# Hybrid mLSTM and gated DeltaNet layer: 512-wide token-major projections, weight units begun from ScalarE's queue, and new places of the chain in TensorE's order

## The chip, the cores and the metric

One core of a Trainium2 chip runs the whole layer as one program. The metric is the device time in microseconds, the median of the runs; less is better.

## The reference, cut to what matters

One decoder layer over 2048 tokens with 1024 features, all in float32. The normalised input is multiplied with one wide input projection. Its columns feed four mLSTM heads (q, k of 128, v, o, z of 256 columns a head) and eight gated DeltaNet heads (q, k, v with a short causal convolution, and a gate z). Both recurrences run chunk by chunk; the outputs are normalised and gated and go through one output projection.

```
h = rms_norm(x, attn_norm); proj = h @ w_in
mq, mk, mv, mo, mz, mi, mf, gqkv, gz, gb, ga = split(proj)
h_m = mlstm_chunkwise(mq, mk, mv, mi, mf)
y_m = rms(h_m) * m_out_norm * sigmoid(mo) * silu(mz)
gq, gk, gv = split(silu(causal_conv(gqkv)))
o_g = gated_delta_chunkwise(l2(gq), l2(gk), gv, log_alpha(ga), sigmoid(gb))
y_g = rms(o_g) * g_out_norm * silu(gz)
out = rms_norm(x + concat(y_m, y_g) @ w_out, final_norm)
```

## The kernel before

The tokens are taken in four segments of 512 (four tiles of 128). Each segment runs eight windows in turn: a P window for each pair of DeltaNet heads (projections gk, gq, gv with the convolution, and gz) and an M window for each mLSTM head (mq and mk, then mv, mo, mz). A projection in float32 is made of three products of rounded parts: weights high and low, input high and low (`hh`, `hl`).

There are two kinds of projection. Feature-major ones (`proj_fm`, names pf_) hold the weights as the stationary operand and stream 512 tokens. Token-major ones (`proj_tm`, names pt_: gz, mv, mo, mz) hold 128 tokens and stream 256 weight columns, one token tile after the other; each tile takes 24 matmuls (8 k by 3 products) into one of three projection banks (`psj`, bufs=3). When a tile is done, ScalarE and VectorE evict it: `gate` in `m_proj` (lines 545 to 547) for mz, line 539 for mo, `keep_v` (lines 528, 536) for mv, `gate` in `g_proj_z` (lines 723, 724) for gz.

TensorE's order is written out by hand. `window` runs through the steps of a window's projections and sums their planned costs; at given shares of the planned total `WIN` it puts in a step of another stream: the DeltaNet preparation (`prep`), the inversion levels (`lvl`, places from `LV0` to `LV1`), the DeltaNet chain (`chain`) and the mLSTM chunks (`mch`). A chunk of the chain has three steps: `sp` (state times key) from which VectorE makes the residual R out of `vr` (line 974); `vq` (line 980), which ScalarE copies to V; and `su` and `op` (lines 991 to 998), from which the state and the output follow. The places of the chain are evenly spaced, six in the P window from `CH0` and the others in the M window from 0.02 to `CH1`. A level's matmuls zp, fp, zq, fq (lines 906 to 932) alternate with copies and transposes (dmz) on the other engines. The other engines' order comes from the framework's list scheduler, in which streams with `PRI` go ahead of the window's own evictions.

The weights are split into high and low parts once, in segment 0, and stored to DRAM. From segment 1 on, `load_w` (line 157) reads them back through SP's queue, four units of 512 KB for a group of 256 columns, into a ring of ten units, one group ahead of use. SP's queue also carries all other loads and the stores of y.

Of the kernel before, what the change touches and what calls it, by code (L numbers as in the profile page):

```python
# [17 lines left out]
P = 128  # L18
# [47 lines left out]
def hybrid_layer(  # L66
# [79 lines left out]
    parts_d = {}  # L146

    def unit(ncol, dt, nm):
        return wp.tile([P, HK, ncol], dt, tag="wu", name=nm, bufs=10)

    def load_w(key, src, ncol, nm, between=None):

        if key in parts_d:
            his, los = ([unit(ncol, F32R, f"{p_}_{nm}_{i}") for i in range(2)] for p_ in ("whi", "wlo"))
            for i in range(2):
                for part, t_ in enumerate((his[i], los[i])):
                    nc.sync.dma_start(t_.bitcast(F32), parts_d[key][part, i])
            return his, los
        return split_w(key, src, ncol, nm, between)

    def split_w(key, src, ncol, nm, between):

        raws = [unit(ncol, F32, f"wraw_{nm}_{i}") for i in range(2)]
        step = 2 if between else HK
        for k in range(0, KT, step):
            nc.sync.dma_start(raws[k // HK][:, k % HK:k % HK + step, :], src[:, k:k + step, :])
# [13 lines left out]
        kept = parts_d[key] = ypool.tile([2, 2, P, HK, ncol], F32, tag=f"wd{nm}", name=f"wd{nm}")  # L180
        for i in range(2):
            for part, t_ in enumerate((his[i], los[i])):
                nc.sync.dma_start(kept[part, i], t_.bitcast(F32))
        return his, los

    wloads = []
    for seg in range(NSEG):
        for kind, n in ORDER_LAST if seg == NSEG - 1 else ORDER:
            for i in range(4) if kind == "M" else (3, 1, 0, 2) if n == 0 else (1, 0, 2, 3):
                nm, key = f"{kind}{seg}_{n}_{i}", (kind, n, i)  # L190
                if kind == "M":
                    wloads.append((key, wg[n * 4 + i], 256, nm))
                elif (n, i) == (0, 3):
                    wloads.append((key, wgz, 256 + NG, nm))
                else:
                    wloads.append((key, wg[16 + n * 4 + i - (n > 0)], 256, nm))
    wready, nloads = [], len(wloads)

    def prefetch_w(between=None):
        if wloads:  # L200
            wready.append(load_w(*wloads.pop(0), between))

# [141 lines left out]
    def proj_fm(w, c0, nm, done):  # L344

        hi, lo = w
        ps = psj.tile([P, T], F32, tag="pj", name=f"pf_{nm}")
        for k in range(KT):
            nc.tensor.matmul(ps, lhsT=hi[k // HK][:, k % HK, c0:c0 + P], rhs=hh[k], start=(k == 0), stop=False)  # L349
            nc.tensor.matmul(ps, lhsT=hi[k // HK][:, k % HK, c0:c0 + P], rhs=hl[k], start=False, stop=False)  # L350
            nc.tensor.matmul(ps, lhsT=lo[k // HK][:, k % HK, c0:c0 + P], rhs=hh[k], start=False, stop=(k == KT - 1))
            if k == KT - 1:
# [3 lines left out]
    def tm_step(ps, w, t, k):  # L356
        hi, lo = (p_[k // HK][:, k % HK, :] for p_ in w)
        ts = slice(t * P, (t + 1) * P)
# [21 lines left out]
    def proj_tm(w, nm, done, scaled=True):  # L380

        n = w[0][0].shape[-1]
        for t in range(NCH):
            ps = psj.tile([P, T], F32, tag="pj", name=f"pt_{nm}_{t}")[:, 0:n]
            for k in range(KT):
                tm_step(ps, w, t, k)
                if k == KT - 1:
                    tm_done(ps, t, done, scaled)
                yield 0.33

    def proj_tm_first(w, nm, done):

        n = w[0][0].shape[-1]
        pss = [psc.tile([P, T], F32, tag="cp", name=f"pt_{nm}_{t}")[:, 0:n] for t in range(NCH)]
        for k in range(KT):
            for t in range(NCH):
                tm_step(pss[t], w, t, k)
            if k == KT - 1:
                rms_first()
# [103 lines left out]

    def m_proj(seg, n, r):
        s_ = f"{seg}_{n}"
        w = next_w()
        qT = wk.tile([P, T], F32, tag="mq", name=f"mq{s_}")
# [4 lines left out]
        r.update(q=qT, k=kT, v=vt, g=G)  # L512
        yield from proj_fm(w, 0, f"mq{s_}",
                           lambda ps: fm_out(qT, ps, DK ** -0.5))
        yield from proj_fm(w, P, f"mk{s_}", lambda ps: fm_out(kT, ps))
        w = next_w()
        if fast:
# [6 lines left out]
        def keep_v(ps, t):  # L524
# [4 lines left out]
            if fast:  # L529
                v_ = vt[:, t, 0:256].bitcast(F32)  # L530
                with tc.high_priority(VPR):
# [3 lines left out]
                    else:  # L535
                        nc.vector.tensor_tensor(vlo[:, t, :], ps, v_, op=ALU.subtract)  # L536
        yield from proj_tm(w, f"mv{s_}", keep_v, False)
        w = next_w()
        yield from proj_tm(w, f"mo{s_}", lambda ps, t: nc.scalar.activation(
            G[:, t, :], ps, AF.Tanh, scale=rs0h[:, t:t + 1] if raw[0] else 0.5), False)  # L540
        w = next_w()

        def gate(ps, t):
# [127 lines left out]
    def g_proj(seg, pr, r, st):  # L671
# [3 lines left out]
        yield from g_proj_qkv(seg, pr, r)  # L675
        if pr:
            yield from g_proj_z(seg, pr, r, st)
# [33 lines left out]

    def g_proj_z(seg, pr, r, st):
        s_ = f"{seg}_{pr}"
        w = next_w()
        G = wkp.tile([P, NCH, 256], F32, tag="gg", name=f"gg{s_}", bufs=2)
# [5 lines left out]
        def gate(ps, t):  # L721
# [4 lines left out]
            if pr == 0:  # L726
# [209 lines left out]
    def g_chain(seg, pr, r, st):  # L936
# [158 lines left out]
    for _ in range(NWARM):  # L1095
        nc.tensor.matmul(warm_ps[:, 0:P], lhsT=ones, rhs=ones, start=True, stop=True)
    lvl, chain, mch = {}, {}, {}
    st = None
    for seg in range(NSEG):
# [17 lines left out]
        for kind, n in ORDER_LAST if last else ORDER:  # L1117
            r = {}
            streams, keep = [], ()
            if kind == "P":  # L1120
# [19 lines left out]
                window(g_proj(seg, n, r, st), WIN, streams, keep)  # L1140
                lvl[n], chain[n] = g_level(seg, n, r), g_chain(seg, n, r, st)
# [3 lines left out]
            else:  # L1145
# [256 lines left out]
```

## Time and profile before

| | |
|---|---|
| median of 3 runs (lowest, highest) | 2298.92 us (2297.42, 2300.68) |
| profiled execution, its time | 2303.72 us |
| its span | 2301.9 us |
| TensorE busy | 2213.8 us, 14798 matmuls |
| VectorE / ScalarE / GpSimd busy | 1837.0 / 854.7 / 796.9 us |
| mean granted TensorE clock | 0.984 |

Busy time is the union of an engine's instructions; matmuls overlap each other, and their ends are modelled. A row of waits gives how long an engine stood idle ahead of an instruction, and whose result ended the wait.

### The profile page before, as it was taken

The numbers are of one execution on the slowest core, as the hardware profiler recorded it, in microseconds if no ns is written. First come the engines' busy times: TensorE is split into PE (matmuls) and PEld (weight loads), VectorE is DVE, ScalarE is ACT, GpSimd is POOL, SyncE is SP. The second block draws the span as 40 slices with busy tenths as digits, with TensorE's granted clock in tenths as the row PEclk, the third lists the DMA queues.
The fourth block names the chain that finished last, engine by engine and source line by source line (L and its number), as shares of the span: only waits on it lengthen the run. The fifth ranks groups of instructions, "written<-read, shape, count | busy, mean of one in ns | idle before, by whom it ended". The sixth has DMA issues, their size and how long they took to land.

```text
span 2301.9 us, 41838 instructions
## 1 busy us (share of the span) xinstructions
PE 2213.8 (96%) x14798; PEld 1965.1 (85%) x14798; DVE 1837.0 (80%) x5168; ACT 854.7 (37%) x2293; POOL 796.9 (35%) x1220
## 2 busy tenths in 40 slices
PE   8899999989999999989999999999999999999998
PEld 7779888887889898979898989888988997788787
DVE  7887878788897979789888898698767737877784
ACT  5445545525242434352424243434244234111111
POOL 4656555652121212421111114221111114555543
PEclk9999999999999999999999999999999999999999
DMA  7766766754546464644454546554546555232321
GB/s 274 257 232 224 248 225 245 256 201 163 191 154 202 144 210 158 229 162 165 145 197 157 199 156 232 167 179 163 181 167 204 174 171 163 73 101 92 101 83 64
DMA packets 183322, 409.19 MB, mean 178 GB/s; under 512 B 51736, under 2 KB 84632, under 8 KB 183112
## 3 DMA queue, kind: packets, MB, share of 16 engines
q1 hardware_dynamic: 182392, 405.74, 51.9%
q8 instruction: 116, 1.90, 0.3%
q14 instruction: 94, 0.77, 0.1%
q10 hardware_dynamic: 720, 0.79, 0.1%
HBM read 309.68 MB, written 96.90 MB: 177 GB/s over the span
## 4 chain that ended last, share of the span: by engine, by line
PE 60%; DVE 24%; DMA 8%; ACT 3%; issue 2%; POOL 2%; SPq 1%; ACTq 0%; POOLq 0%; DVEq 0%
PE po L1258 5%; PE po L1257 5%; PE po L1256 5%; DVE xb L850 3%; DVE tb L846 3%; DVE kw L500 2%; DVE ktok L500 2%; PE pt_gz L361 2%; PE pt_gz L359 2%; PE pt_gz L360 2%; PE pt_mz L359 2%; PE pt_mz L360 2%; PE pt_mz L361 2%; PE pf_gv L349 2%; PE pf_gv L350 2%
## 5 line engine op out<-in xcount | busy, mean ns | idle before, releaser
L1217 DVE STREAM_TRANSPOSE ytt<-yl 32x256 f32<-32x256 f32 x448 | 195.3, 436 | 45.3 <-POOL ylo L1185 39.3
L1014 POOL TENSOR_TENSOR gms<-gms,nhalf 128x2 f32<-128x2 f32 x64 | 47.4, 740 | 410.9 <-DVE gms L1012 408.6
L846 DVE TENSOR_TENSOR tb<-xb,lbt 128x248 f32<-128x248 f32 (+30 forms) x496 | 167.1, 337 | 20.7 <-DMA lbt<-l_d 7.9
L850 DVE TENSOR_TENSOR xb<-xb,tb 128x248 f32<-128x248 f32 (+30 forms) x496 | 168.4, 339 | 12.8
L359 PE MATMUL pt_mv<-whi_M,hh 128*128 128x256 f32 x512 | 150.7, 294 | 8.3 <-DVE mk L371 3.9
L359 PE MATMUL pt_gz<-whi_P,hh 128*128 128x256 f32 (+1 forms) x512 | 152.6, 298 | 4.3 <-ACT hh L337 2.5
L359 PE MATMUL pt_mz<-whi_M,hh 128*128 128x256 f32 x512 | 149.6, 292 | 3.1 <-DVE tz L546 3.1
L359 PE MATMUL pt_mo<-whi_M,hh 128*128 128x256 f32 x512 | 148.7, 290 | 3.2 <-DVE vlo L536 3.2
L361 PE MATMUL pt_gz<-whi_P,hl 128*128 128x256 f32 (+1 forms) x512 | 147.8, 289 | 1.6 <-DVE hl L338 1.6
L360 PE MATMUL pt_gz<-wlo_P,hh 128*128 128x256 f32 (+1 forms) x512 | 147.7, 288 | 1.7 <-DVE wlo_P L178 1.7
L360 PE MATMUL pt_mv<-wlo_M,hh 128*128 128x256 f32 x512 | 147.2, 287 | 0.0
L361 PE MATMUL pt_mv<-whi_M,hl 128*128 128x256 f32 x512 | 146.9, 287 | 0.0
L360 PE MATMUL pt_mz<-wlo_M,hh 128*128 128x256 f32 x512 | 145.4, 284 | 0.0
L361 PE MATMUL pt_mz<-whi_M,hl 128*128 128x256 f32 x512 | 145.3, 284 | 0.0
L360 PE MATMUL pt_mo<-wlo_M,hh 128*128 128x256 f32 x512 | 144.2, 282 | 0.0
L361 PE MATMUL pt_mo<-whi_M,hl 128*128 128x256 f32 x512 | 144.2, 282 | 0.0
L1265 ACT ACTIVATE jkf<-xr 128x512 f32<-128x512 f32 (+1 forms) x33 | 20.4, 619 | 271.5 <-DVE xr L1263 148.1
L1256 PE MATMUL po<-woh,yh 128*128 128x512 f32 (+1 forms) x297 | 114.6, 386 | 1.6 <-ACT yh L1183 1.6
L1258 PE MATMUL po<-woh,ylo 128*128 128x512 f32 (+1 forms) x297 | 114.7, 386 | 0.1
L178 POOL TENSOR_TENSOR wlo_M<-wraw_M,whi_M 128x256 fp32r<-128x256 f32 x128 | 97.4, 793 | 49.3 <-ACT whi_M L175 48.7
L1257 PE MATMUL po<-wol,yh 128*128 128x512 f32 (+1 forms) x297 | 114.3, 385 | 0.0
L359 PEld LDWEIGHTS pt_mv<-whi_M,hh 128*128 128x128 f32 x512 | 100.0, 195 | 10.5 <-DVE mk L371 4.3
(408 smaller groups left out, 7539.4 us busy)
## 6 DMA issues: line engine op xcount, KB each, us to landing
whi_M<-wdM SPq DMA_DIRECT2D x96, 512.0 KB, 4.1
wlo_M<-wdM SPq DMA_DIRECT2D x96, 512.0 KB, 5.2
whi_P<-wdP SPq DMA_DIRECT2D x90, 512.0 KB, 3.9
wlo_P<-wdP SPq DMA_DIRECT2D x90, 512.0 KB, 4.7
wraw_M<-in_wg_dram SPq DMA_DIRECT2D x32, 512.0 KB, 5.9
wdM<-whi_M SPq DMA_DIRECT2D x32, 512.0 KB, 3.2
wdM<-wlo_M SPq DMA_DIRECT2D x32, 512.0 KB, 5.2
wraw_P<-in_wg_dram SPq DMA_DIRECT2D x30, 512.0 KB, 5.6
```

What stands on the lines that cost most here:

```text
L178: eng.tensor_tensor(lo[:, ks, :], raw_[:, ks, :], hi[:, ks, :].bitcast(F32), op=ALU.subtract)
L359: nc.tensor.matmul(ps, lhsT=hh[k][:, ts], rhs=hi, start=(k == 0), stop=False)
L360: nc.tensor.matmul(ps, lhsT=hh[k][:, ts], rhs=lo, start=False, stop=False)
L361: nc.tensor.matmul(ps, lhsT=hl[k][:, ts], rhs=hi, start=False, stop=(k == KT - 1))
L500: nc.vector.transpose(dst[32 * a:32 * a + 32, :, 32 * b:32 * b + 32], s4[32 * b:32 * b + 32, :, a, :])
L846: nc.vector.tensor_tensor(tb[:, :, 0:n], xb[:, :, i:i + 1].broadcast_to([P, 8, n]), lbt[:, i:i + 1, i + 1:32].broadcast_to([P, 8, n]), op= ...
L850: nc.vector.tensor_tensor(xs, xs, tb[:, :, 0:n], op=ALU.subtract)
L1014: nc.gpsimd.tensor_tensor(ms, ms, nhalf[:, 0:2], op=ALU.pow)
L1217: nc.vector.transpose(ytt[32 * b:32 * b + 32, :, 32 * a:32 * a + 32], y3[32 * a:32 * a + 32, :, 32 * b:32 * b + 32])
L1256: nc.tensor.matmul(ps, lhsT=yh, rhs=woh, start=(k == 0), stop=False)
L1257: nc.tensor.matmul(ps, lhsT=yh, rhs=wol, start=False, stop=False)
L1258: nc.tensor.matmul(ps, lhsT=ylo, rhs=woh, start=False, stop=(k == 15))
```

## The change

Four things are done. (1) From segment 1 on, mo and mz of a head are one projection of 512 columns, and, for the seven head pairs of `wide_z`, gz and mv too; gz then leaves the P window and stands with mv at the start of the M window, ahead of mq and mk. `proj_tm_wide` takes two token tiles at a time, k in the outer loop, into two of the three banks. The planned window lengths become 31.0 (P) and 52.0 (M) where gz moves. The paired weights are stored side by side in DRAM. (2) From segment 1 on, weight units are loaded by ScalarE's queue, each where TensorE's order has just released a unit of the ring (`pump`, `freed`). (3) The places of levels, chain, last mLSTM steps and gate steps are given one by one: longer gaps behind steps that VectorE follows, shorter behind those that ScalarE follows. (4) The chain's residual R is written in the place of `vr`, which gets two buffers.

```diff
-LV0, LV1, CH0, CH_N, CH1 = (0.26, 0.42, 0.44, 6, 1.0)
+NU = 10
+LVP, LVW = (0.26, 0.3, 0.34, 0.4, 0.45), (0.2, 0.24, 0.29, 0.34, 0.41)
+CHP = (0.42, 0.46, 0.63, 0.71, 0.88)
+CHM = (0.03, 0.11, 0.28, 0.45, 0.53, 0.7, 0.87, 0.95)
+CWP = (0.44, 0.5, 0.7, 0.82)
+CWM = (0.01, 0.15, 0.22, 0.36, 0.5, 0.57, 0.71, 0.85, 0.92)
-MC2 = (0.0, 0.1, 0.15, 0.195, 0.2)
+MC2 = (0.0, 0.1, 0.18, 0.25, 0.32)
-GP, RB = ((0.4, 0.9, 0.97), 0.31)
+GP, RB = ((0.4, 0.82, 0.97), 0.31)
-LVA = (0.26, 0.45, 0.47, 1.03)
+LVA = ((0.26, 0.3, 0.345, 0.41, 0.46), 0.47, 1.03)
...
+        if isinstance(key, list):
+            w = Weights(nm, 512, 2)
+            kept = parts_d[key[0]][0]
+            w.due = [((p_, i), kept[p_, i // 2, :, i % 2 * 2:i % 2 * 2 + 2]) for i in range(4) for p_ in range(2)]
+        else:
+            kept, c0, n = parts_d[key]
+            w = Weights(nm, n, HK)
             for i in range(2):
-                for part, t_ in enumerate((his[i], los[i])):
-                    nc.sync.dma_start(t_.bitcast(F32), parts_d[key][part, i])
-            return his, los
-        return split_w(key, src, ncol, nm, between)
+                for p_ in range(2):
+                    w.due.append(((p_, i), kept[p_, i, :, :, c0:c0 + n]))
+        return w
+
+    def pump():
+        while coming and ring["free"] > 0:
+            w = coming[0]
+            at, src = w.due.pop(0)
+            t_ = w.units[at] = unit_(w.rows, w.n, F32R, f"w{at[0]}_{w.nm}_{at[1]}")
+            nc.scalar.dma_start(t_.bitcast(F32), src)
+            ring["free"] -= 1
+            if not w.due:
+                wready.append(coming.pop(0))
+
+    def freed(n):
+        ring["free"] += n
+        if not wloads:
+            pump()
...
+                nc.sync.dma_start(kept[part, i, :, :, c0:c0 + ncol], t_.bitcast(F32))
...
+    WIDE = [[("M", n, 2), ("M", n, 3)] for n in range(4)] + [[("P", n, 3), ("M", n, 1)] for n in range(1, 4)]
+
+    def wide_z(seg, n):
+        return seg > 0 and n > 0 and not (seg == NSEG - 1 and n > 1)
...
+                coming.extend(get_w(*g_) for g_ in wgets)
+                ring["free"] = NU - 8
...
+            if c0 and k % HK == HK - 1:
+                freed(2)
...
+    def proj_tm_wide(w, nm, done):
+        for t0 in range(0, NCH, 2):
+            pss = [psj.tile([P, T], F32, tag="pj", name=f"pt_{nm}_{t0 + i}") for i in range(2)]
+            for k in range(KT):
+                for i in range(2):
+                    tm_step(pss[i], w, t0 + i, k)
+                    if t0 and i and k % 2:
+                        freed(2)
+                    if k == KT - 1:
+                        done(pss[i], t0 + i)
+                    yield 0.65
...
+        def gates(ps, t):
+            nc.scalar.activation(G[:, t, :], ps[:, 0:256], AF.Tanh, scale=0.5)
+            gate(ps[:, 256:512], t)
+
+        if wide_z(seg, n):
+            z_gate = g_gate(seg, n, rp, None)
+
+            def both(ps, t):
+                z_gate(ps, t)
+                keep_v(ps[:, 256:512], t)
+            yield from proj_tm_wide(next_w(), f"mv{s_}", both)
+        w = next_w()
+        yield from proj_fm(w, 0, f"mq{s_}",
+                           lambda ps: fm_out(qT, ps, DK ** -0.5))
+        yield from proj_fm(w, P, f"mk{s_}", lambda ps: fm_out(kT, ps))
+        if not wide_z(seg, n):
+            yield from proj_tm(next_w(), f"mv{s_}", keep_v, False)
+        w = next_w()
+        if seg:
+            yield from proj_tm_wide(w, f"mo{s_}", gates)
+            return
...
-            vr = sm.tile([P, 2, P], F32, tag="vr", name=f"vr{n_}", bufs=1)
+            vr = sm.tile([P, 2, P], F32, tag="vr", name=f"vr{n_}", bufs=2)
...
-            vr = nxt
+            R = nxt
...
-            R = sm.tile([P, 2, P], F32, tag="R", name=f"R{n_}", bufs=1)
-            if first:
-                nc.scalar.copy(R, vr)
-            else:
+            if not first:
...
-                    vr[:, j, :], op0=ALU.mult, op1=ALU.add)
+                    R[:, j, :], op0=ALU.mult, op1=ALU.add)
...
-    WIN = 41.6
+    WIN, WINP, WINM = 41.6, 31.0, 52.0
...
+    def win(kind, seg, n):
+        return WIN if not wide_z(seg, n) else WINP if kind == "P" else WINM
...
-                    streams += [(lvl[q], NLV, LV0, LV1, PRI), (chain[q], CH_N, CH0, 1.01, PRI)]
+                    streams += [(lvl[q], LVW if wide_z(seg, n) else LVP, None, None, PRI),
+                                (chain[q], CWP if wide_z(seg, n) else CHP, None, None, PRI)]
...
-                        streams.append((chain[(n - 1) % 4], NCS - CH_N, 0.02, CH1, PRI))
+                        streams.append((chain[(n - 1) % 4], CWM if wide_z(seg, n) else CHM,
+                                        None, None, PRI))
```

## Rows read from the trace of the kernel before

**Rows 1.** The page's first part: busy us, share of the span, instructions.

```profile
span 2301.9 us, 41838 instructions
...
PE 2213.8 (96%) x14798; PEld 1965.1 (85%) x14798; DVE 1837.0 (80%) x5168; ACT 854.7 (37%) x2293; POOL 796.9 (35%) x1220
```

**Rows 2.** Busy time by stretch: one P window, one M window, and their sum.

```profile
622.30:679.80 57.50, 56.64 (x406) 49.12 (x405) 52.12 (x156) 27.33 (x71) 11.44 (x23) 1.00 0.45 157
679.80:735.40 55.60, 54.91 (x419) 52.56 (x418) 44.93 (x157) 14.54 (x53) 9.85 (x14) 1.00 0.57 194
sum 113.10, PE 111.55 PEld 101.68 DVE 97.05 ACT 41.86 POOL 21.29; mean PE 55.77 PEld 50.84 DVE 48.52 ACT 20.93 POOL 10.64
```

**Rows 3.** TensorE's waits by releaser: us in total, times, longest us.

```profile
PE vq L980 <- DVE R L974: 22.5, 16, 3.5
PE zq L926 <- DVE dmz L921: 6.0, 7, 2.1
PE lbp L455 <- DVE cq L451: 4.9, 2, 3.3
...
PE zp L906 <- DVE dmz L900: 3.0, 2, 1.8
PE nd L613 <- DVE CN L646: 2.6, 3, 1.8
```

**Rows 4.** TensorE's timeline, 256 columns wide: start, us, instruction; 36 rows left out.

```profile
1199.53 0.28 PE L359 MATMUL pt_mz<-whi_M,hh 128*128 128x256 f32 x1
...
1203.91 0.28 PE L360 MATMUL pt_mz<-wlo_M,hh 128*128 128x256 f32 x1
```

**Rows 5.** TensorE's timeline, 512 columns wide; 12 rows left out.

```profile
1240.68 0.39 PE L350 MATMUL pf_gv<-hl,whi_P 128*128 128x512 f32 x1
...
1243.67 0.39 PE L351 MATMUL pf_gv<-hh,wlo_P 128*128 128x512 f32 x1
```

**Rows 6.** Groups by line and shape of evictions: busy us, mean ns, idle before.

```profile
L539 ACT ACTIVATE mg<-pt_mo 128x256 f32<-128x256 f32 x48 | 18.3, 381 | 79.0 <-PE pt_mo L361 78.8
L545 ACT ACTIVATE tz<-pt_mz 128x256 f32<-128x256 f32 x64 | 24.7, 385 | 52.9 <-PE pt_mz L361 47.4 <-DVE mg L547 2.7 <-DVE tb L846 2.5
L546 DVE SCALAR_TENSOR_TENSOR tz<-tz,pt_mz 128x256 f32<-128x256 f32 x64 | 26.7, 417 | 14.2 <-ACT tz L545 14.0
L724 DVE SCALAR_TENSOR_TENSOR gg<-gtz,pt_gz 128x256 f32<-128x256 f32 x64 | 26.5, 414 | 13.7 <-ACT gtz L723 13.5
L536 DVE TENSOR_TENSOR vlo<-pt_mv,mv 128x256 fp32r<-128x256 f32 x28 | 11.7, 419 | 2.9 <-ACT mv L528 2.7
```

**Rows 7.** Timeline of ScalarE and VectorE around one eviction of gz.

```profile
678.42 3.13 DVE L500 STREAM_TRANSPOSE gv<-xingv 32x128 f32<-32x128 f32 x10
...
679.00 0.36 ACT L723 ACTIVATE gtz<-pt_gz 128x256 f32<-128x256 f32 x1
...
681.77 1.90 DVE L500 STREAM_TRANSPOSE gv<-xingv 32x128 f32<-32x128 f32 x6
...
683.70 0.42 DVE L724 SCALAR_TENSOR_TENSOR gg<-gtz,pt_gz 128x256 f32<-128x256 f32 x1
```

**Rows 8.** Timeline around one eviction of mz.

```profile
1200.12 0.28 PE L361 MATMUL pt_mz<-whi_M,hl 128*128 128x256 f32 x1
...
1200.44 0.39 ACT L545 ACTIVATE tz<-pt_mz 128x256 f32<-128x256 f32 x1 [0.64 <-PE pt_mz L361]
...
1200.86 0.42 DVE L546 SCALAR_TENSOR_TENSOR tz<-tz,pt_mz 128x256 f32<-128x256 f32 x1 [0.51 <-ACT tz L545]
```

**Rows 9.** The waits of SP's own queue.

```profile
SPq L157 <- PE pf_gq L351: 151.7, 21, 16.7
...
SPq L157 <- PE pf_gk L351: 79.2, 22, 11.6
```

**Rows 10.** ScalarE's waits by releaser.

```profile
ACT vr L952 <- DVE R L974: 85.6, 27, 10.0
...
ACT gyt L1010 <- DMA yd<-yt: 26.5, 10, 3.4
```

**Rows 11.** Stores of y by line 667: duration of an issue on ScalarE's queue, ns minimum/median/maximum.

```profile
L667 ACTq DMA_DIRECT2D yd<-yt x4: 326/326/343, 1914.3 to 1942.6; - x4
```

More of the change, by code (lines that the diff above doesn't have):

```diff
@@ L146, in hybrid_layer, with unit_, __init__, part @@
     parts_d = {}
+    def unit_(rows, ncol, dt, nm):
+        return wp.tile([P, rows, ncol], dt, tag="wu", name=nm, bufs=NU)
     def unit(ncol, dt, nm):
[L149 to L154, printed above, removed]
-            for i in range(2):
-                for part, t_ in enumerate((his[i], los[i])):
-                    nc.sync.dma_start(t_.bitcast(F32), parts_d[key][part, i])
-            return his, los
-        return split_w(key, src, ncol, nm, between)
+        return unit_(HK, ncol, dt, nm)
+    class Weights:
+        def __init__(self, nm, ncol, rows):
+            self.nm, self.n, self.rows, self.units, self.due = nm, ncol, rows, {}, []
+        def part(self, p_, k):
+            return self.units[p_, k // self.rows][:, k % self.rows, :]
+    ring = {"free": NU}
+    coming = []
+    def get_w(key, nm):
+        if isinstance(key, list):
[5 more added lines that the diff above has]
+            w = Weights(nm, n, HK)
+            for i in range(2):
+                for p_ in range(2):
[14 more added lines that the diff above has]
+            pump()
     def split_w(key, src, ncol, nm, between):
@@ L179, in split_w @@
                     lo[:, ks, :], raw_[:, ks, :], hi[:, ks, :].bitcast(F32), op=ALU.subtract)
-        kept = parts_d[key] = ypool.tile([2, 2, P, HK, ncol], F32, tag=f"wd{nm}", name=f"wd{nm}")
+        pair = next((p_ for p_ in WIDE if key in p_), None)
+        c0 = pair.index(key) * ncol if pair else 0
+        if c0:
+            kept = parts_d[pair[0]][0]
+        else:
+            kept = ypool.tile([2, 2, P, HK, 512 if pair else ncol], F32, tag=f"wd{nm}", name=f"wd{nm}")
+        parts_d[key] = kept, c0, ncol
+        w = Weights(nm, ncol, HK)
         for i in range(2):
             for part, t_ in enumerate((his[i], los[i])):
-                nc.sync.dma_start(kept[part, i], t_.bitcast(F32))
-        return his, los
-    wloads = []
+                w.units[part, i] = t_
+                nc.sync.dma_start(kept[part, i, :, :, c0:c0 + ncol], t_.bitcast(F32))
+        return w
+    WIDE = [[("M", n, 2), ("M", n, 3)] for n in range(4)] + [[("P", n, 3), ("M", n, 1)] for n in range(1, 4)]
+    def wide_z(seg, n):
+        return seg > 0 and n > 0 and not (seg == NSEG - 1 and n > 1)
+    wloads, wgets = [], []
     for seg in range(NSEG):
@@ L200, in prefetch_w @@
         if wloads:
-            wready.append(load_w(*wloads.pop(0), between))
+            wready.append(split_w(*wloads.pop(0), between))
+            if not wloads:
+                coming.extend(get_w(*g_) for g_ in wgets)
+                ring["free"] = NU - 8
     def next_w():
@@ L344, in proj_fm @@
     def proj_fm(w, c0, nm, done):
-        hi, lo = w
         ps = psj.tile([P, T], F32, tag="pj", name=f"pf_{nm}")
         for k in range(KT):
-            nc.tensor.matmul(ps, lhsT=hi[k // HK][:, k % HK, c0:c0 + P], rhs=hh[k], start=(k == 0), stop=False)
-            nc.tensor.matmul(ps, lhsT=hi[k // HK][:, k % HK, c0:c0 + P], rhs=hl[k], start=False, stop=False)
-            nc.tensor.matmul(ps, lhsT=lo[k // HK][:, k % HK, c0:c0 + P], rhs=hh[k], start=False, stop=(k == KT - 1))
+            hi, lo = (w.part(p_, k)[:, c0:c0 + P] for p_ in range(2))
+            nc.tensor.matmul(ps, lhsT=hi, rhs=hh[k], start=(k == 0), stop=False)
+            nc.tensor.matmul(ps, lhsT=hi, rhs=hl[k], start=False, stop=False)
+            nc.tensor.matmul(ps, lhsT=lo, rhs=hh[k], start=False, stop=(k == KT - 1))
+            if c0 and k % HK == HK - 1:
+                freed(2)
             if k == KT - 1:
@@ L356, in tm_step @@
     def tm_step(ps, w, t, k):
-        hi, lo = (p_[k // HK][:, k % HK, :] for p_ in w)
+        hi, lo = (w.part(p_, k) for p_ in range(2))
         ts = slice(t * P, (t + 1) * P)
@@ L380, in proj_tm @@
     def proj_tm(w, nm, done, scaled=True):
-        n = w[0][0].shape[-1]
+        n = w.n
         for t in range(NCH):
@@ L397, in proj_tm_first @@
                 tm_step(pss[t], w, t, k)
+            if k % HK == HK - 1:
+                freed(2)
             if k == KT - 1:
@@ L512, in m_proj @@
         r.update(q=qT, k=kT, v=vt, g=G)
[L513 to L516, printed above, removed]
         if fast:
@@ L675, in g_proj @@
         yield from g_proj_qkv(seg, pr, r)
-        if pr:
+        if pr and not wide_z(seg, pr):
             yield from g_proj_z(seg, pr, r, st)
@@ L712, in g_proj_z, with g_gate @@
     def g_proj_z(seg, pr, r, st):
+        gate = g_gate(seg, pr, r, st)
+        yield from (proj_tm_first if seg == 0 and pr == 0 else proj_tm)(next_w(), f"gz{seg}_{pr}", gate)
+    def g_gate(seg, pr, r, st):
         s_ = f"{seg}_{pr}"
-        w = next_w()
         G = wkp.tile([P, NCH, 256], F32, tag="gg", name=f"gg{s_}", bufs=2)
@@ L730, in gate @@
                     beta[:, t, :], ps[:, 272:280], -1.0, 85.0, op0=ALU.mult, op1=ALU.min)
-        yield from (proj_tm_first if seg == 0 and pr == 0 else proj_tm)(w, f"gz{s_}", gate)
+        return gate
     def g_prep(seg, pr, r, st):
```

34 lines of the change are left out of this document (21 added, 13 removed).

## Prediction

> **What bounds the kernel now.** I read the page's first part, then the busy times of one regular pair of windows, then TensorE's waits by releaser. TensorE is busy for 2213.8 of 2301.9 us [rows 1]. That share flatters it, because a matmul's modelled end overlaps the next start, so the waits say more: 88.1 us of the span hold no matmul, the five groups of waits shown have 39.0 us of them, and the largest is 22.5 us at the second product of the DeltaNet chain, waiting for VectorE's residual R [rows 3]. In the regular pair (one P window, one M window) TensorE is busy 111.55 of 113.10 us, VectorE 97.05, ScalarE 41.86 [rows 2]. So the kernel is bound by TensorE's columns, with VectorE close behind (86%) and ScalarE at 37%. A microsecond taken off TensorE counts in full as long as VectorE keeps up; no wait of TensorE ends on a weight load.
>
> **The change, part by part.**
>
> *The rate of wide matmuls.* In segments 1 to 3 the 12 pairs mo/mz and 7 pairs gz/mv become 512 wide: 2304 + 1344 = 3648 matmuls of 256 columns become 1824 of 512 (19 x 4 tiles x 8 k x 3). Between the two rows of the narrow stretch lie 37 intervals in 4.38 us, 118.4 ns each, so a pair takes 236.8 ns [rows 4]; between those of the 512-wide stretch 13 intervals in 2.99 us, 230.0 ns [rows 5]. The gain is 6.8 ns x 1824 = 12 us. The Trainium skill, page "TensorE: Matmul & The Clock Gate", section "Back-to-back issue gap", gives N / 2.4 GHz + 2.5 ns: by it a pair would save 2.5 ns, and this part 5 us instead of 12. The row has 11.7 ns over the pure column time at 256 columns and 16.7 at 512, not 2.5, so the row decides.
>
> *The chain's places.* A chunk of the chain is sp (VectorE makes R from it), vq (ScalarE copies V), su. The old places were even, 0.14 of an M window apart; the new ones leave 0.17 after sp and 0.08 after vq. An M window lasts 55.6 us [rows 2], so R gets 0.03 x 55.6 = 1.7 us more. The 16 waits for R have a mean of 1.4 us, the longest 3.5 [rows 3]: the mean one disappears, the longest keeps 1.8. I take 18 us back of 22.5; bounds 8 (order of VectorE's queue moves with it) and 22.5. V's gap shrinks from 0.14 to 0.08 of the window, 4.4 us, against a copy that I estimate at 0.4 us from the passes of the same 128x256 shape [rows 6]: 0.
>
> *The levels' and gates' places.* zq waits 6.0 us and zp 3.0 for dmz [rows 3]. The third gap grows from 0.04 to 0.06 in unwidened windows; in the widened ones the shorter window gives it back. I take 3 of 9, bounds 0 and 9. lbp waits 4.9 us for cq, twice [rows 3]; its second step moves from 0.90 to 0.82 while the third stays at 0.97, so cq gets 0.08 of a 57.5 us window, 4.6 us more, against a longest wait of 3.3: 5 back, bounds 0 and 5. The wider places of the last mLSTM steps (0.18, 0.25, 0.32) give CN more time: 2 of 2.6, bounds 0 and 2.6.
>
> *Two banks at a time.* The wide projection fills two of the three projection banks and needs two more in the middle. From the modelled end of the first tile to the first matmul that writes into its bank again there are 7 starts of 230 ns less the 390 ns of that last matmul: 1.22 us. In this time ScalarE does two passes (381 and 385 ns for mo/mz) and VectorE one (417) or, for gz/mv, two (414 and 419) [rows 6]. Undisturbed, mz's eviction starts 0.04 us after its matmul's end and VectorE ends at 1201.28, 0.88 us after it [rows 8]; with one more ScalarE pass 1.26, a stall of 0.04 us. Disturbed, it is far more: in the shown gz tile ScalarE began at 679.00 and VectorE ended at 684.12 after sixteen transposes of the gv convolution (the end of 3.13 and the 1.90 us block) [rows 7]. That is 5.1 us late, 5.5 with a further pass, a stall of 4.3 us. Before the change two more tiles of 24 x 118.4 ns covered it; now 1.22 us do.
> The 12 mo/mz boundaries lie at about 0.8 of the M window, where the mz row stands: 0.5 us each, 6 us (bounds 0.04 and 1.5 each: 0.5 to 18). The 7 gz/mv boundaries come some 14 us into the M window (10.4 planned, with prep's products between), and that window now follows the gv convolution directly, since gz no longer stands between. Its transposes and prep are both on VectorE then, as in the late row; but part of ScalarE's and VectorE's lateness there comes from waits that the change removes (next part). I take the middle of 0.04 and 4.3, 2.2 each, 15 us (0.3 to 30).
>
> *Loads begun from ScalarE.* 384 loads (3 segments x 32 groups x 4 units) leave SP's queue. They cost SP waits of 151.7 + 79.2 us in the two largest groups alone [rows 9], and y's stores queue behind them: ScalarE waits 26.5 us in ten pieces for such stores [rows 10]. These waits go, off TensorE's path, so I price them at 0 directly. On ScalarE each issue takes 326 ns [rows 11]: 384 x 0.326 = 125 us over segments 1 to 3, two at a time, 0.65 us. In a pair of windows that adds 32 x 0.326 = 10.4 us at most to 41.86 of 113.1: room is left. Queued behind an issue that waits for a matmul are the evictions and V copies of later matmuls; V's 4.4 us cover one pair. I take 2 us; bounds 0 and 30 (rival 2). Storing and reading the paired weights in 1 KB runs instead of 4 KB is off every wait of TensorE in the list and is read a segment later: 0.
>
> *The residual in vr's place.* One small tile goes, vr gets two buffers. ScalarE's 85.6 us of waits of vr for R [rows 10] end. They were mostly time in which the chain waited for R anyway, so 0; it also frees ScalarE for evictions, which is why I don't take the upper end above.
>
> **Sum.** Gains 12 + 18 + 3 + 5 + 2 = 40 us; costs 6 + 15 + 2 = 23 us; together -17 us. The profiled execution took 2303.7 us (span 2301.9 and 1.8 around it), 4.8 above the median of the runs; 2303.7 - 17 = 2286.7 on its own scale, 2282 on that of the runs, 0.7% less.
>
> **Rivals.**
> 1. *The third bank decides: slower.* If VectorE evicts gz/mv as late as in [rows 7], 7 x 4.3 = 30 us, and mo/mz lose 1.5 each, 18 us; if the chain's places give back only their lower bound (8 of 18), and the levels nothing, gains are 12 + 8 + 5 = 25 and the result is 2299 + 50 - 25 = 2324; with the gains of the sum 2309. It decides from a mean stall of 40/19 = 2.1 us at the 19 boundaries. For it: VectorE is busy 52.12 of 57.5 us in the P window [rows 2], and the same work but gz's now falls to a window shorter by 4 x 24 x 118.4 ns = 11.4 us. Against it: mz's place is calm, and evictions may be ordered ahead of the transposes. The Trainium skill, page "Perfetto Trace Analysis", section "Matmuls", wants independent groups to rotate through banks so that one's evacuation overlaps the next's matmuls, and also calls larger matmuls more efficient; here the two halves of its rule stand against each other, and [rows 4, 5] price only the second.
> 2. *ScalarE is held by its issues: slower or even.* An issue waits for the matmul that frees its unit, as SP's did. If one of four of the 192 pairs holds up a chain step that TensorE waits for, 48 x 0.65 = 31 us go: 2282 + 29 = 2311. Against it: they are begun where the unit becomes free, not a group ahead as on SP.
> 3. *No change.* Stalls of 2 us at all 19 boundaries (38 + 2) cancel the 40: 2299.
> 4. *All covers hold.* With ScalarE and SP freed, evictions are prompt: costs of 1 + 2, gains of 45: 2257.
>
> **Chances.** The forecast (-5 to -30 us, 2269 to 2294 by itself) 0.52; rival 4 0.12; rival 3 0.10; rival 1 0.19; rival 2 0.07. A kernel of this length can be told from another at about 0.2%, 4.6 us. Faster 0.64, same 0.10, slower 0.26. The range takes in rival 4 below and most of rivals 1 and 2 above: 2254 to 2316.
>
> **What would show it.** Right: wide matmuls at 230 ns starts; vq's wait for R under 6 us; waits of TensorE at mo/mz under 8 us and at gz/mv near 15, on VectorE; whole pair of windows near 112 us. SP free of waits for TensorE. Wrong: waits of TensorE of several us in the middle of every gz/mv pair, ended by gg or vlo (rival 1); new waits on ScalarE (V, or an eviction) with an issue before them (rival 2); wide matmuls at 236 ns or more (no gain of rate).

## The result, and the profile after

The changed kernel is slower: median 2380.01 us of 4 runs (2377.33 to 2389.4) against 2298.93, ratio 1.036 with a 95% interval of 1.033 to 1.0389. That is 81 us more where 17 less were forecast, and beyond the range's upper end of 2316.

The page's first part, after (span, then busy time, share and count), answers [rows 1]:

```profile
span 2377.5 us, 38109 instructions
...
PE 2222.8 (93%) x12974; PEld 1890.9 (80%) x12974; DVE 1860.5 (78%) x5168; ACT 852.1 (36%) x2289; POOL 803.7 (34%) x1220
```

TensorE has 1824 matmuls fewer, as forecast, but the span without a matmul grew from 88.1 us to 2377.5 - 2222.8 = 154.7. TensorE's waits by releaser (total, times, longest us) say where, beside [rows 3]:

```profile
PE pt_mv L430 <- DVE vlo L621: 32.6, 6, 8.1
PE pt_mo L430 <- DVE tz L625: 21.7, 7, 6.8
PE zp L1013 <- DVE dmz L1007: 15.0, 7, 8.2
PE pt_mv L430 <- ACT mv L613: 12.5, 2, 6.3
...
PE vq L1085 <- DVE vr L1079: 4.7, 2, 4.0
```

The wait that the new places aimed at, vq's for the residual, fell from 22.5 to 4.7 us. In its place stand waits in the wide projections, named pt_mv (gz and mv; the narrow mv has the same name, with 4.1 us of the first row) and pt_mo (mo and mz), for VectorE: rival 1's sign. Its regular pair of windows, busy times by stretch beside [rows 2], and three pieces of its M window:

```profile
614.70:663.40 48.70, 45.63 (x306) 37.78 (x305) 43.35 (x128) 25.75 (x72) 11.42 (x23) 1.00 0.43 139
663.40:740.70 77.30, 69.08 (x325) 57.55 (x324) 59.80 (x195) 18.27 (x55) 10.71 (x15) 0.93 0.50 165
678.60:685.40 6.80, 0.46 (x2) 0.05 (x2) 6.62 (x22) 2.00 (x7) 0.19 (x1) 0.84 0.29 80
685.40:690.00 4.60, 4.59 (x17) 4.21 (x18) 3.40 (x12) 1.48 (x6) 1.41 (x2) 0.50 0.44 113
690.00:697.00 7.00, 7.00 (x32) 5.68 (x31) 5.37 (x17) 0.25 (x2) 0.86 (x1) 1.00 0.84 275
```

The pair takes 126.0 us in place of 113.1. In the third row TensorE is idle for 6.3 of 6.8 us while VectorE is busy for 6.62. In the fourth it works, but at a granted clock of 0.50 (1.2 GHz); 1.00 comes back in the fifth. Right behind the other five waits of 6.2 to 8.1 us in the middle of gz/mv pairs the granted clock is 0.50 too. So each long wait is paid twice. The mean granted clock is 0.970 against 0.984: with only two levels, time at the lower one is 2 x (1 - mean) x span, about 143 us against 74, and a TensorE that works through that time loses half of it.

The timeline around that wait shows who held the bank (columns as in [rows 7]):

```profile
677.70 0.38 ACT L830 ACTIVATE gtz<-pt_mv 128x256 f32<-128x256 f32 x1 [1.70 <-PE pt_mv L432]
677.94 0.88 DVE L935 SCALAR_TENSOR_TENSOR ua<-kk,scol,ua 128x256 f32<-128x256 f32 x2
...
678.39 0.39 ACT L830 ACTIVATE gtz<-pt_mv 128x256 f32<-128x256 f32 x1 [0.31 <-PE pt_mv L432]
678.66 0.40 PE L432 MATMUL pt_mv<-w_V,hl 128*128 128x512 f32 x1
678.83 3.48 DVE L589 STREAM_TRANSPOSE gv<-xingv 32x128 f32<-32x128 f32 x11
682.34 0.88 DVE L935 SCALAR_TENSOR_TENSOR ua<-kk,scol,ua 128x256 f32<-128x256 f32 x2
...
683.13 0.74 DVE L831 SCALAR_TENSOR_TENSOR gg<-gtz,pt_mv 128x256 f32<-128x256 f32 x2
683.58 0.70 ACT L613 CAST mv<-pt_mv 128x256 fp32r<-128x256 f32 x2 [4.80 <-DVE gg L831]
...
684.84 0.75 DVE L621 TENSOR_TENSOR vlo<-pt_mv,mv 128x256 fp32r<-128x256 f32 x2
...
685.41 0.77 PE L430 MATMUL pt_mv<-w_V,hh 128*128 128x512 f32 x1 [6.35 <-DVE vlo L621]
```

ScalarE's first pass is prompt. VectorE then does eleven transposes of the gv convolution before its own first pass, gg, at 683.13. ScalarE's second pass, mv, needs nothing of gg, yet it waits 4.80 us for it; only then vlo runs and the bank is free. The Trainium skill, page "PSUM — Partial Sum Buffer", section "PSUM bank collisions raise a hardware error", says that the compiler's scheduler orders any two instructions of different engines that touch one bank and quadrant, reads among them; the row agrees. So four passes stand in turn, with VectorE's lateness in the middle.

The matmuls' rate came as forecast. Between these two starts of the changed kernel lie 27 intervals in 6.25 us, 231.5 ns each (230.0 was taken from [rows 5]):

```profile
690.37 0.39 PE L430 MATMUL pt_mv<-w_V,hh 128*128 128x512 f32 x1
...
696.62 0.40 PE L430 MATMUL pt_mv<-w_V,hh 128*128 128x512 f32 x1
```

In the same stretch ScalarE starts six loads of weights, and the next eviction, gtz, stands behind them in its queue:

```profile
691.03 6.37 ACTq L193 DMA_DIRECT2D w_M<-wdM  x6
...
698.92 0.40 PE L432 MATMUL pt_mv<-w_V,hl 128*128 128x512 f32 x1
...
699.41 0.39 ACT L830 ACTIVATE gtz<-pt_mv 128x256 f32<-128x256 f32 x1 [9.16 <-DMA w_M<-wdM]
```

The row puts ScalarE's 9.16 idle us down to a load, but gtz starts 0.09 us after the end of its tile's last matmul (698.92 + 0.40): it had nothing to evict before, and the loads cost nothing here. Rival 2 has to be looked for elsewhere. As forecast, SP's waits for TensorE at loads [rows 9] and ScalarE's 85.6 us of vr for R [rows 10] are no longer in the lists of waits.

### The profile page after: what moved, and what is told of

It reads as the page before. It is cut to its first block, busy times and chain, and to the rows that moved or that the text cites. A ratio compares the mean times of both kernels' runs of the same rounds, so it can differ in the third digit from the quotient of the medians.

```text
span 2377.5 us, 38109 instructions
## 1 busy us (share of the span) xinstructions
PE 2222.8 (93%) x12974; PEld 1890.9 (80%) x12974; DVE 1860.5 (78%) x5168; ACT 852.1 (36%) x2289; POOL 803.7 (34%) x1220
## 4 chain that ended last, share of the span: by engine, by line
PE 51%; DVE 34%; DMA 6%; ACT 3%; issue 3%; POOL 2%; SPq 1%; ACTq 0%; POOLq 0%; DVEq 0%
PE po L1369 5%; PE po L1367 5%; PE po L1368 5%; DVE tb L953 4%; DVE xb L957 4%; DVE gv L589 4%; DVE ktok L589 3%; PE pt_mo L430 3%; PE pt_mo L431 3%; PE pt_mo L432 3%; DVE kw L589 2%; DVE ua L935 2%; PE pt_mv L430 2%; PE pf_gk L418 1%; DVE gv L800 1%
## 5 line engine op out<-in xcount | busy, mean ns | idle before, releaser
L430 PE MATMUL pt_mo<-w_M,hh 128*128 128x512 f32 x384 | 159.9, 416 | 27.0 <-DVE tz L625 21.7
L431 PE MATMUL pt_mo<-w_M,hh 128*128 128x512 f32 x384 | 152.9, 398 | 0.0
L432 PE MATMUL pt_mo<-w_M,hl 128*128 128x512 f32 x384 | 152.7, 398 | 0.0
L430 PE MATMUL pt_mv<-w_V,hh 128*128 128x512 f32 x224 | 94.5, 422 | 41.0 <-DVE vlo L621 28.5
L220 POOL TENSOR_TENSOR wlo_P<-wraw_P,whi_P 128x256 fp32r<-128x256 f32 x104 | 88.1, 875 | 61.0 <-ACT whi_P L217 60.7
L1331 POOL TENSOR_TENSOR ytt<-ytt,gain_c 128x256 f32<-128x256 f32 x120 | 82.9, 720 | 69.7 <-DVE ytt L1328 66.8
L800 DVE SCALAR_TENSOR_TENSOR gk<-xingk,conv_c,gk 128x512 f32<-128x512 f32 x96 | 74.0, 771 | 36.3 <-ACT gk L797 34.6
L1296 POOL TENSOR_TENSOR ylo<-ytt,yh 128x256 fp32r<-128x256 f32 x120 | 85.0, 744 | 16.4 <-ACT yh L1294 16.4
L589 DVE STREAM_TRANSPOSE ktok<-gk 32x128 f32<-32x128 f32 x288 | 87.1, 302 | 4.2
L431 PE MATMUL pt_mv<-w_V,hh 128*128 128x512 f32 x224 | 90.3, 403 | 0.0
L589 DVE STREAM_TRANSPOSE gv<-xingv 32x128 f32<-32x128 f32 x288 | 86.9, 302 | 4.3
L432 PE MATMUL pt_mv<-w_V,hl 128*128 128x512 f32 x224 | 90.1, 402 | 0.0
```

The source lines that it names most:

```text
L220: eng.tensor_tensor(lo[:, ks, :], raw_[:, ks, :], hi[:, ks, :].bitcast(F32), op=ALU.subtract)
L430: nc.tensor.matmul(ps, lhsT=hh[k][:, ts], rhs=hi, start=(k == 0), stop=False)
L431: nc.tensor.matmul(ps, lhsT=hh[k][:, ts], rhs=lo, start=False, stop=False)
L432: nc.tensor.matmul(ps, lhsT=hl[k][:, ts], rhs=hi, start=False, stop=(k == KT - 1))
L589: nc.vector.transpose(dst[32 * a:32 * a + 32, :, 32 * b:32 * b + 32], s4[32 * b:32 * b + 32, :, a, :])
L800: nc.vector.scalar_tensor_tensor(d, xi[:, tap:tap + T], conv_c[:, fi, tap:tap + 1], d, op0=ALU.mult, op1=ALU.add)
```

## The experiments

Three theories stood at the start: the bank wait (rival 1); ScalarE held by its issues (rival 2); and lateness that only moves, to the levels and the weight loads, when one wait is taken away. Each time below is a median; its ratio is to the kernel before on the same chip, with the 95% interval. The kernel before took 2296 to 2298 us on each of these chips, so times of different chips are compared to about 2 us.

**One token tile after the other** in the wide projections, so that the third bank is free while one is evicted.

```diff
-        for t0 in range(0, NCH, 2):
-            pss = [psj.tile(...) for i in range(2)]
+        for t in range(NCH):
+            ps = psj.tile(...)
             for k in range(KT):
...
-                    if t0 and i and k % 2:
+                if t == NCH - 1 and k % 2:
                     freed(2)
```

> The wide projection takes one token tile after the other instead of two at a time, so that two more tiles of 24 x 230 ns, 11 us, stand between a bank's last product and its next first one; nothing else of the change is touched. Theory A (the bank that TensorE needs again after 1.22 us sets the loss): TensorE's waits in pt_mv and pt_mo for vlo, mv and tz fall from some 72 us to under 10, the stretches at the half clock shrink from 147 us towards 80, and the time falls to 2290 to 2310 us. Theory B (ScalarE is held by its load issues): no change, 2365 to 2385 us. Theory C (VectorE has too much to do in the window behind the gv convolution, and its lag only moves): the waits go to other lines of the same window, 2345 to 2375 us.

2370.24 us, 1.0319 (1.0299 to 1.0338). The bank waits are gone, and only 10 us with them. Its waits of TensorE show new ones, for the levels and for weights:

```profile
PE zp L1012 <- DVE dmz L1006: 43.8, 10, 7.3
...
PE pf_mq L420 <- DMA w_M<-wdM: 7.5, 6, 2.2
```

So rival 1's wait alone did not explain the 81 us.

**gz and mv narrow again**, in their old places; mo and mz stay wide in pairs.

```diff
-        return seg > 0 and n > 0 and not (seg == NSEG - 1 and n > 1)
+        return False
```

> No gz/mv pair is widened: gz goes back to the end of the P window and mv behind mk, 256 wide; mo/mz stay 512 wide in pairs of tiles. Theory A: the 45 us of waits in the middle of gz/mv go with the half clock behind them, those in the middle of mo/mz stay: 2305 to 2325 us. Theory B: nearly as slow as the change, 2360 to 2380 us. Theory C: as theory A or a little less, 2300 to 2320 us, so that this run alone does not tell A from C.

2319.26 us, 1.0094 (1.0077 to 1.011): 61 of the 81 us hang on gz/mv. The edit also gives the P window its length and its levels' places back, so it does not part the bank from the levels.

**Loads from SyncE** (SP's queue), all else as in the changed kernel.

```diff
-            nc.scalar.dma_start(t_.bitcast(F32), src)
+            nc.sync.dma_start(t_.bitcast(F32), src)
```

> The weight units are begun from SP's queue at the same places of the program instead of ScalarE's. Theory A: within 10 us of the change, 2370 to 2390 us. Theory B: 60 us or more come back, 2300 to 2330 us.

2384.05 us, 1.0375 (1.0358 to 1.0391): no gain here. If the issues cost anything in this kernel, other waits hide it; without those they do cost (below).

**The wide evictions with the chain's priority.**

```diff
             def both(ps, t):
-                z_gate(ps, t)
-                keep_v(ps[:, 256:512], t)
+                with tc.high_priority(PRI):
+                    z_gate(ps, t)
+                    keep_v(ps[:, 256:512], t)
```

> The evictions of gz/mv get the priority of the chain and the preparation, so that VectorE takes them ahead of the convolution's transposes; banks and tile order stay those of the change. Theory A with VectorE's order as the cause of the lag: the middle waits in gz/mv fall from 6 to 8 us to 1 to 2 us, the time to 2335 to 2355 us. Theory B: no change. Theory C: the transposes are late instead, and their readers wait: 2360 to 2380 us.

2378.36 us, 1.035 (1.0333 to 1.0366). gg still came behind the transposes in VectorE's queue; the scheduler's order did not change there, so the run says nothing against the bank wait.

**mo/mz wide one tile after the other, gz/mv narrow**, with loads from ScalarE and from SyncE (the edits above, combined).

> gz and mv narrow and in their old places, mo/mz 512 wide, one token tile after the other; ScalarE's loads, the new places and the residual in vr's place stay. Of the 21 us that the kernel with mo/mz in pairs of tiles (e2_gz_back) loses against the kernel before, theory A (the bank wait) puts 16.3 us of waits for tz and some half clock on the pairs: 2295 to 2305 us. Theory C (VectorE's lag only moves): 2312 to 2320 us, with other waits in their place.

> The same with the loads begun from SP's queue. In the last segment the kernels with ScalarE's loads wait some 7 to 8 us for dmz in an M window and need 200 to 203 us from the last P window on, the one with SP's loads 188.6. If ScalarE's queue is the cause there (theory B, in that stretch alone), 10 to 14 us less than e5: 2283 to 2292 us. If not: the same as e5 within 4 us.

2326.25 us, 1.0131 (1.0118 to 1.0144), and 2310.27, 1.0064 (1.0048 to 1.0079). With the gz/mv waits out, the queue is worth 16 us.

**Nothing widened**, ScalarE's loads, new places and the residual kept; and **the new places alone** in the kernel before.

```diff
-    WIDE = [[("M", n, 2), ("M", n, 3)] for n in range(4)] + ...
+    WIDE = []
...
-        if seg:
+        if False:
             yield from proj_tm_wide(w, f"mo{s_}", gates)
```

> Nothing is widened: mo, mz, gz and mv are 256 wide in the order of the kernel before; ScalarE's loads, new places and the residual in vr's place stay. Rate of wide matmuls worth 7.8 us for mo/mz (1152 x 6.8 ns): this kernel 8 us slower than e5 if e5 has no new waits, 2303 to 2313 us. If the wide form brings other costs even tile by tile: the same as e5 or faster.

> The kernel before with the new places of levels, chain, last mLSTM steps and gate steps alone. The prediction's terms for them: 18 + 3 + 5 + 2 = 28 us less, 2270 us. Rival: the waits go to the next steps or VectorE's order, 2293 to 2303 us. The waits of vq for R fall from 22.5 to under 6 us in both.

2327.11 us, 1.0137 (1.012 to 1.0153), and 2290.15, 0.9973 (0.9962 to 0.9983). The places alone give 6 us. These waits of TensorE in the kernel with the places alone say why not 28:

```profile
PE pt_mv L361 <- DVE vlo L538: 13.7, 7, 3.4
PE pt_mz L361 <- DVE tz L548: 6.9, 4, 2.9
...
PE vq L982 <- DVE R L976: 4.8, 2, 3.9
```

and in the kernel before:

```profile
PE pt_mz L359 <- DVE tz L546: 3.1, 4, 1.2
...
PE pt_mv L359 <- DVE vlo L536: 0.7, 2, 0.5
```

vq's wait fell by 17.7 us and lbp's by 4.3 [rows 3], but at mv's banks TensorE now waits 13.7 us for vlo in place of 0.7, and at mz's 6.9 in place of 3.1: more than half of the gain went into other waits for the same engine.

**Nothing widened, loads from SyncE; the places with the residual** in vr's place.

> The kernel with nothing widened (2327 us, 1.0137 of before), but the units of weights begun from SyncE's queue again; the order of the units, the new places and the residual stay. If ScalarE held at its issues is what costs there (rival 2), this loses the 16 us that the same edit gave with mo/mz wide: 2308 to 2313. If the order in which units are begun, or the residual's place, is the cost, it stays at 2320 to 2330. If both, something between, and the remainder over 2290 (the places alone) is those two together.

> The kernel before with the new places (2290 us alone) and, on top, the residual written in the scaled values' place, the scaled values in two buffers. The prediction priced that at nothing: 2290, within 4 us. If it costs, this goes to 2300 to 2320, and that is the share of the 37 us that lie between the new places alone and the kernel with nothing widened.

2289.71 us, 0.9968 (0.9955 to 0.998): the queue alone is worth 37 us here, more than the 16 that its expectation took over from the run with mo/mz wide. And 2285.19, 0.9944 (0.9932 to 0.9957), the fastest of all: the residual was priced at nothing and gives about 5 us. Here is the narrow kernel that loads from ScalarE, ahead of an mLSTM step:

```profile
809.30 0.83 ACTq L193 DMA_DIRECT2D w_M<-wdM  x2
...
811.87 0.39 PE L420 MATMUL pf_mk<-hh,w_M 128*128 128x512 f32 x1
...
816.08 0.88 DVE L665 SCALAR_TENSOR_TENSOR ptt<-nm,ccol,negmask 128x128 f32<-128x128 f32 x3 [4.10 <-DMA nm<-rows]
816.52 0.69 ACT L667 ACTIVATE nm<-nm,mprev 128x128 f32<-128x128 f32 x2 [8.48 <-DMA w_M<-wdM]
...
817.48 1.40 ACTq L193 DMA_DIRECT2D w_M<-wdM  x1
818.91 0.59 ACT L438 COPY mk<-pf_mk 128x512 f32<-128x512 f32 x1 [1.41 <-PE pt_mv L432]
```

ScalarE is idle for 8.48 us, but only the first 2.1 (to 810.13) pass at the two loads; then nm waits for VectorE's step ptt, which waits for nm's own rows. The hold by a load is the later one: mk's last matmul ended at 812.26, and its copy, behind nm in the queue, then stands another 1.40 us behind a load that waits until a matmul of pt_mv frees its unit. TensorE's waits grow most at the levels. With loads from ScalarE:

```profile
PE zp L1013 <- DVE dmz L1007: 13.5, 7, 7.3
...
PE fp L1022 <- ACT dmz L1017: 9.8, 5, 2.2
```

With loads from SyncE they are 3.2 and 4.2 us. How the holds lead there was not followed. The Trainium skill, page "DMA: Bandwidth & Descriptors", section "Issuing engines are not separate DMA queues", says that starting transfers on several engines saves only the sequencer's time to initiate them; here nothing saved on SP's queue shows, and 37 us were lost with the loads on ScalarE's.

**One tile after the other, levels back in time**: the shortened P window's levels and first chain steps at the planner's times that they have in a full one.

```diff
-LVW = (0.2, 0.24, 0.29, 0.34, 0.41)
+LVW = (0.35, 0.4, 0.456, 0.537, 0.604)
-CWP = (0.44, 0.5, 0.7, 0.82)
+CWP = (0.564, 0.618, 0.75, 0.85)
```

> The changed kernel with one token tile after the other (2370 us), and the levels and the chain's first steps in the shortened P windows set back to where they stand in time in a P window of full length (levels at 10.9 to 18.7 us of the planner's time in place of 6.2 to 12.7, chain at 17.5 to 26). If the 44 us of levels that wait for the substitution's loads in that kernel are what took the place of the bank waits, they go and the time falls to 2325 to 2340, the time with only mo/mz wide. If the half clock and the units held longer carry the loss, it stays at 2355 to 2375.

2337.97 us, 1.0184 (1.0168 to 1.0199): 32 us back.

**The same with SyncE; then also in pairs again; and mo/mz alone wide in pairs with SyncE.**

> The changed kernel with one token tile after the other, the levels back at their place in time (2338 us together) and the units begun from SyncE. If ScalarE held at its issues is the next share, the 16 us (mo/mz wide) to 37 us (nothing widened) that this edit gave elsewhere come off: 2301 to 2322. If it was hidden here behind other waits, 2330 to 2338.

> The same with the token tiles in pairs again, as in the changed kernel: the bank wait alone is put back. If that wait and the half clock behind it cost what the trace of the changed kernel shows in the middle of the gz/mv pairs (six waits of 6.2 to 8.1 us), this is 30 to 45 us over the kernel with one tile after the other, 2335 to 2365. If most of the wait came from ScalarE held at its issues and from the early levels, both mended here, the two agree within 12 us.

> mo and mz wide in pairs, gz and mv narrow (2319 us), the units begun from SyncE. Nothing widened and SyncE gave 2290, so: if widening mo/mz gains its 6 us by the matmuls' rate, 2284; if it costs as it did with one tile after the other (2310), 2300 to 2312; ScalarE's share by the earlier pair of runs would leave 2303.

2307.48 us, 1.0042 (1.003 to 1.0054); 2353.14, 1.0232 (1.0207 to 1.0258); 2302.84, 1.0019 (1.0007 to 1.003). The first two differ in the order of the tiles alone: 46 us for the bank wait, with both other causes out. It is a net figure, because one tile after the other also frees the ring's units later (below). The waits of the kernel in pairs:

```profile
PE pt_mv L430 <- DVE vlo L621: 37.3, 7, 7.9
PE pt_mo L430 <- DVE tz L625: 15.4, 6, 5.6
PE pt_mv L430 <- ACT mv L613: 11.6, 2, 5.8
```

and of the kernel with one tile after the other:

```profile
PE pf_mq L418 <- DMA w_M<-wdM: 14.5, 6, 3.1
...
PE pt_gz L430 <- DMA w_P<-wdP: 6.2, 2, 4.2
...
PE zp L1012 <- DVE dmz L1006: 3.1, 2, 1.9
```

Here zp's wait has gone from 43.8 to 3.1 us (26.3 with the levels back and ScalarE's loads). What is left is the wait for weights, most of it at mq: a wide group holds eight of the ring's ten units, and this order releases them only in its last tile.

**gz/mv alone wide**, one tile after the other, late levels, SyncE; mo and mz narrow.

> gz and mv wide, one token tile after the other, levels back in time, units begun from SyncE; mo and mz narrow as before. Widening mo/mz cost 13 us in pairs (2303 against 2290) and 20 one after the other (2310 against 2290), so leaving them narrow should take those 20 us off the 2307 of the same kernel with mo/mz wide: 2284 to 2292. Under 2284 the widening of gz/mv pays beyond nothing; over 2295 the two losses were not independent.

2312.68 us, 1.007 (1.005 to 1.0091), 23 us over nothing widened. The losses do not add: widening mo/mz costs 13 (in pairs) or 21 us, gz/mv 23, both together 18.

**Who holds the bank.** Pairs, late levels, SyncE; ScalarE's two passes first; then also VectorE's passes without reading the bank (`tz` and `v_` stand in place of `ps`, so the kernel leaves z out of the gate and the low part of v is zero). The diff is that of the second.

```diff
-                z_gate(ps, t)
-                keep_v(ps[:, 256:512], t)
+                nc.scalar.activation(tz, ps[:, 0:256], AF.Tanh, scale=0.5)
+                nc.scalar.copy(vt[:, t, 0:256], ps[:, 256:512])
+                with tc.high_priority(PRI):
+                    nc.vector.scalar_tensor_tensor(rp["g"][:, t, :], tz, 1.0, ps[:, 0:256], ...)
+                    nc.vector.tensor_tensor(vlo[:, t, :], ps[:, 256:512], v_, op=ALU.subtract)
```

> The kernel with pairs, late levels and SyncE's loads (2353 us), its two passes of ScalarE over a wide bank put ahead of VectorE's two, which have the chain's priority. If the four passes in turn (ScalarE, VectorE, ScalarE, VectorE) are what keeps the bank, each mid-pair wait is shorter by one change of engine, 1 to 2 us: 2335 to 2347. If VectorE's other work ahead of its first pass is what keeps it, VectorE still comes late and the time stays at 2347 to 2355.

> The same, but VectorE's two passes read no bank: the gate is formed from the tanh alone and the low part of v from its high part (it is zero), so this leaves out z in the gate and v's low part; the passes themselves stay. ScalarE alone frees the bank. If VectorE's place in the bank's release is the whole of the wait, the mid-pair waits fall to under 1 us and the time to that of one tile after the other, 2300 to 2315. If ScalarE is late as well, 2325 to 2345.

2341.88 us, 1.0201 (1.0185 to 1.0217). The order of passes is worth 11 us of the 46 by the medians and 7 by the ratios, whose intervals overlap; the edit also gives VectorE's passes the chain's priority, which alone had brought nothing in the changed kernel. The longest mid-pair wait of gz/mv is 6.6 us in place of 7.9:

```profile
PE pt_mv L430 <- DVE vlo L644: 24.6, 4, 6.6
...
PE pt_mv L430 <- DVE gg L641: 11.1, 2, 5.8
```

And 2333.8, 1.0163 (1.0148 to 1.0179), when ScalarE alone frees the bank: the mid-pair waits of gz/mv are gone, but it is not 2307, and ScalarE is not late either. The wait has moved to mo/mz, 40.0 us in place of 15.4, and 8.7 us for weights are new:

```profile
PE pt_mo L430 <- DVE tz L625: 40.0, 7, 10.4
PE pf_mq L420 <- DMA w_M<-wdM: 8.7, 6, 2.5
```

One of the waits at mo/mz, in the timeline:

```profile
717.92 0.24 DVE L960 TENSOR_TENSOR tb<-xb,lbt 128x80 f32<-128x80 f32 x1
...
722.27 0.18 DVE L960 TENSOR_TENSOR tb<-xb,lbt 128x16 f32<-128x16 f32 x1
722.36 0.41 DVE L625 SCALAR_TENSOR_TENSOR tz<-tz,pt_mo 128x256 f32<-128x256 f32 x1
...
722.83 0.79 PE L430 MATMUL pt_mo<-w_M,hh 128*128 128x512 f32 x1 [6.05 <-DVE tz L625]
```

VectorE runs the substitution's chain of small steps, and mz's pass comes behind it. A bank that needs VectorE at a fixed moment finds it busy with one or the other of its serial jobs.

## Why the prediction was wrong

Step by step from the changed kernel, with one edit each: SyncE 2384, levels back 2353, one tile after the other 2307, nothing widened 2290, loads a group ahead as before 2285, residual out 2290, old places 2296. The shares hold for this order: one tile after the other as the first edit gave 10 us, not 46, because the levels' waits grew in its place.

**Two banks at a time: the step that failed.** It took 2.2 us for each gz/mv boundary, 4.3 at most, and 0.5 for mo/mz. Measured were six waits of 6.2 to 8.1 us in the middle of gz/mv pairs and up to 6.8 at mo/mz, and in sum 46 us (2353 against 2307) where 21 were forecast. Three things were left out. VectorE's two passes were added up as if ScalarE's second ran beside them; the passes stand in turn, worth 7 to 11 us. The window that loses gz brings the gv transposes directly ahead of the boundary, which the text saw, but then took half of what its own late row showed [rows 7]. And each wait is followed by a stretch at 1.2 GHz. Rival 1 had the place and the sign; its price, 2324, was too low.

**The levels' places: a gain of 3 was taken, 31 to 32 were lost** (2370 to 2338 with one tile, 2384 to 2353 in pairs). In the shortened P window the levels stand at 6.2 to 12.7 us of planned time, not 10.9 to 18.7, and zp and zq wait for the substitution: with one tile after the other, VectorE sits idle for 44.9 us in all ahead of its step dmz (L1006), which zp needs, until E, the substitution's result, has landed. The text looked at the gaps between the levels, not at the first one's distance from what it needs.

**Loads from ScalarE: priced 2, rival 2 at 31.** In the changed kernel itself the queue costs nothing that can be seen (2380 against 2384), hidden, if it is there, behind the other waits. Where those are out or smaller it costs 16 us (mo/mz wide), 31 (both wide, levels back) and 37 (nothing widened). Rival 2's 31 was about right as a price. The argument against it, that loads begin where the unit is free, holds for TensorE's written order and not for ScalarE's, whose finished copy mk stood 1.40 us behind a load in the shown rows. That the queue costs this much is shown by the edit that changes nothing else; how such holds reach TensorE is open.

**The chain's places: 28 us forecast with lbp, levels and last steps, 6 measured.** The waits named went as forecast; 13 us came back at mv's evictions and 4 at mz's, for the same engine.

**The rate: right** in the matmul starts, 231.5 against 236.8 ns, 10 us. No variant shows it as time: with SyncE's loads and the levels at their old time, widening still costs 13 to 23 us. With both projections wide, one tile after the other, the weights' wait of 17.6 us in two rows of pf_mq and the lower clock behind it are large enough to explain the loss. With mo/mz alone wide, one tile after the other, they are not: TensorE waits 3.4 us for weights there, and 12.0 at zp where 3.2 stand with nothing widened. In pairs, mo/mz alone still wait 17.3 us for banks. What would be left of the rate with a larger ring or a fourth bank is open; neither was tried.

**The residual's place:** priced 0, gives about 5 us.

## What to carry to other kernels

A wider tile that leaves one bank fewer to rotate turns VectorE's lateness, nearly harmless before, into TensorE's waits; price it with the latest eviction that the trace shows and with every reader of the bank in turn. When a piece of work leaves a window, all that is placed by shares of the window moves in time against what it waits for. Loads that must wait for a buffer belong on a queue of an engine with nothing else to do.

## What the runs showed of the hardware

TensorE's granted clock falls behind waits of a few microseconds. In the kernel with one tile after the other, late levels and SyncE's loads, TensorE works 0.74 of 3.80 us, and the next 3.40 run at 0.50 (1.2 GHz), in this table of its stretches:

```profile
690.30:694.10 3.80, 0.74 (x3) 0.30 (x2) 3.60 (x11) 0.00 (x0) 0.00 (x0) 1.00 0.88 323
694.10:697.50 3.40, 2.87 (x7) 2.29 (x8) 3.19 (x10) 0.37 (x1) 0.00 (x0) 0.50 1.02 405
```

After the 6.35 us wait of the changed kernel the matmuls of 512 columns start 0.43 to 0.56 us apart (from 685.41 on), where 0.23 is usual:

```profile
685.97 0.63 PE L431 MATMUL pt_mv<-w_V,hh 128*128 128x512 f32 x1
686.40 0.63 PE L432 MATMUL pt_mv<-w_V,hl 128*128 128x512 f32 x1
```

Time at 1.2 GHz, worked out as above from the mean clocks 0.981 and 0.970, is about 88 us with one tile after the other (2307) and 141 in pairs (2353): of the 46 us between them up to 27 are the clock's, the rest the waits'.
